# Squaring the MLP's features twice on ScalarE, and scaling the second pair of each group on VectorE, in a one-step hybrid diffusion layer

## The chip, the cores and the metric

The kernel runs on one core of a Trainium2 chip. The metric is the device time of one execution in microseconds (us); lower is better. Times from several runs are given as a median.

## What is computed

One transformer-like layer is run for two groups of tokens that share the weights: 512 latent tokens and 128 context tokens, 640 in all, each of width 1024. The layer has a modulated norm, a combined projection, two parallel head groups (mLSTM and latent attention), an output projection, and an MLP. The change lies in the MLP alone:

```python
h2 = _rmsnorm(x, norm2_g) * (1 + sc2) + sh2
x = x + g2 * (jnp.square(jax.nn.relu(h2 @ w_mlp_up)) @ w_mlp_down)   # 1024 -> 4096 -> 1024
```

## The kernel before

Tokens lie along the free dimension and features along the 128 partitions, so a block of 128 features of all tokens is a tile of 128x640, worked on in two halves of 320 tokens. All data are float32. A matmul operand is written as a high part (rounded to `fp32r`) and a low part (what the rounding left), and a product is three matmul passes: high by high, high by low, low by high.

The MLP goes through 4096 hidden features in 8 groups (`g`) of two pairs (`p = 2g` and `2g + 1`); a pair is two blocks of 128 features. For each pair `up_pair` forms the up product by a seven-product scheme (M1 to M7, each 12 matmuls of 128x322 in `product`, line 1232). Each product lands in one of four small PSUM buffers, and VectorE adds it into the pair's tiles `r1`, `r2`, `u` (line 1248; M1 is copied by ScalarE, line 1253). A PSUM buffer is free for a later product only when VectorE has read it.

`up_out` (lines 1265 to 1277) then makes the pair's features, half block by half block, four of them in a pair. The token's norm factor is multiplied in on GpSimd (line 1270), ScalarE adds the bias and applies relu (line 1274, one or two instructions, since the two token groups have different biases), ScalarE squares into the high part `fh` (line 1275), VectorE squares the same tile in place at full precision (line 1276), and VectorE subtracts the high part from that to get the low part `fl` (line 1277).

When both pairs of a group are there, eight down tiles `dn` of 24 matmuls each follow (line 634, called from the loop at the end), and VectorE adds them into the residual (`gated`, lines 1115 to 1117). The first of the eight takes all terms with `fh` first and those with `fl` last (`low_last`). The first products of the next group's pair are placed in between.

Weights come by DMA on SyncE's queue; each is split into its high part on ScalarE (line 109) and its low part on VectorE (line 110). GpSimd also forms the sums `S` of weight quarters that the seven-product scheme wants (line 219). So VectorE, ScalarE and GpSimd each have one queue, in order, in which feature work, weight work and PSUM reading share the places.

The order in each queue isn't the order of the code: the tile framework schedules the whole program at build time by a timeline of its own, and it may also alternate the matmuls of two products that are open at the same time. A change of engine therefore moves neighbours too.

Of the kernel before, what the change touches and what calls it, by code (L numbers as in the profile page):

```python
# [13 lines left out]
AF = mybir.ActivationFunctionType  # L14
ALU = mybir.AluOpType
# [39 lines left out]
def hybrid_layer(ctx: ExitStack, tc: tile.TileContext, d, o):  # L55
    nc = tc.nc
    V, S, G, PE = nc.vector, nc.scalar, nc.gpsimd, nc.tensor
# [17 lines left out]
    def U(name, dt=F32):  # L75
        return upool.tile([P, UNIT], dt, tag="u", name=name)
# [12 lines left out]
    def Tt(name, dt=F32, n=T):  # L89
        t = tp.tile([P, 646], dt, tag="t", name=name)  # L90
        return t[:, :n]
# [13 lines left out]
    def f(ap):  # L105
        return ap.bitcast(F32)
# [238 lines left out]
    for what in ORD:  # L345
        if what == "x":
            i = state["x"]
            nc.sync.dma_start(out=x3[i // 2][:, 2 * (i % 2):2 * (i % 2) + 2], in_=d["x"][:, 2 * i:2 * i + 2])
            state["x"] += 1
        elif what == "a":  # L350
            t = view(U(f"ad{len(adu)}"), 0, 4, 512)
# [111 lines left out]
    for g in range(4):  # L463
        if g:
            ada_first(g)
        if g == 1:
            rbs = Tt("rb1")
# [57 lines left out]
    for i in range(NT):  # L525
# [7 lines left out]
                      in_=st[:, KL + ROPE:KL + ROPE + 8].rearrange("p (a b) -> p a b", a=2))  # L533
        V.tensor_copy(out=gf[:, i, :].rearrange("p (a b) -> p a b", a=2)[:, :, 0:4],
                      in_=st[:, KL + ROPE + 8:KL + ROPE + 16].rearrange("p (a b) -> p a b", a=2))
# [48 lines left out]
    for ci, row in enumerate((r_a, r_e, r_w)):  # L584
        nt = NT if ci < 2 else 4
        pc = psS(f"pcol{ci}")
        for i in range(nt):
            PE.transpose(out=pc[:, i * 64:(i + 1) * 64], in_=row[:, i * P:(i + 1) * P], identity=ident[0:64, 0:64])
        V.tensor_copy(out=cols[:, ci, 0:nt].rearrange("p t d h -> p (t d) h"),
                      in_=pc[:, 0:nt * 64].rearrange("p (t b) -> p t b", b=32)[:, :, 0:4])  # L590
# [8 lines left out]
    for w in range(2):  # L599
# [4 lines left out]
                        in1=gs.unsqueeze(1).broadcast_to([P, NT, 2, 16]), op=ALU.mult)  # L604
# [195 lines left out]
    for k in range(2):  # L800
        pt = psD(f"ckt{k}")
        for i in range(NT):
# [17 lines left out]
                    in0=krn[:, 0:4].rearrange("p t (a b) -> p t a b", a=2)[:, :, ::-1, :],  # L820
                    in1=sg_[:, 1, 0:4].rearrange("p t (a b) -> p t a b", a=2), op=ALU.mult)
# [9 lines left out]
    for hf in range(2):  # L831
# [7 lines left out]
        for i in range(6):  # L839
            ps = psD(f"kvu{hf}{i}")[:, 0:512]  # L840
            for k in range(2):
                c = slice(k * 512, (k + 1) * 512)
# [13 lines left out]
        for i in range(6):  # L856
            G.tensor_tensor(out=kn[:, i, :, 0:NOPE], in0=kn[:, i, :, 0:NOPE], in1=rsk[:, i, :].unsqueeze(2).broadcast_to([P, 4, NOPE]), op=ALU.mult)
            G.tensor_tensor(out=kn[:, i, :, NOPE:QK], in0=krr[:, i:i + 1, :].broadcast_to([P, 4, ROPE]),
                            in1=rsk[:, i, :].unsqueeze(2).broadcast_to([P, 4, ROPE]), op=ALU.mult)
# [12 lines left out]
    for hf in range(2):  # L872
# [4 lines left out]
        for i in range(NT):  # L877
            ps = (psS if i % 2 else psD)(f"qu{hf}{i}")
            for k in range(3):
                hi, lo = w0 if k < 2 else w1  # L880
                c = slice((k % 2) * QL, (k % 2) * QL + QL)
# [7 lines left out]
            if i < 4:  # L889
                rt = view(Pp(f"rt{hf}{i}"), 0, 4, ROPE)  # L890
                V.tensor_tensor(out=rt.rearrange("p h (a b) -> p h a b", a=2),
                                in0=p4[:, :, NOPE:QK].rearrange("p h (a b) -> p h a b", a=2)[:, :, ::-1, :],
                                in1=sg_[:, 0, i:i + 1, :].rearrange("p t (a b) -> p t a b", a=2).broadcast_to([P, 4, 2, 16]), op=ALU.mult)
# [260 lines left out]
    for m in OUT_ORDER:  # L1154
# [19 lines left out]
        if m < 4:  # L1174
            osplit("B11", m, z1)
            t = Pp(f"t1{m}", n=SW)
            G.tensor_tensor(out=t, in0=z2, in1=z1, op=ALU.subtract)
            osplit("T1", m, t)
        else:
            k = m - 4  # L1180
            E = V if k == 3 else G
            t = Tt(f"t32{m}", n=2 * SW)
            t3, t2 = t[:, 0:SW], t[:, SW:2 * SW]
            c = TL - HT
# [52 lines left out]
    held = {}  # L1237
# [24 lines left out]
            if p == 0 and name == "M7":  # L1262
                add("M5", m5)

    def up_out(r, rbs, FH, FL):

        for n, hf in ((0, 0), (1, 1), (1, 0), (0, 1)):
            c = slice(hf * HT, (hf + 1) * HT)
            t = r[n][:, 2 + hf * HT:2 + (hf + 1) * HT]
            G.tensor_tensor(out=t, in0=t, in1=rbs[:, c], op=ALU.mult)  # L1270
            for w, (c0, c1) in enumerate(((0, TL), (TL, T))):
                c0, c1 = max(c0 - hf * HT, 0), min(c1 - hf * HT, HT)
                if c1 > c0:
                    S.activation(out=t[:, c0:c1], in_=t[:, c0:c1], func=AF.Relu, bias=r[n][:, w:w + 1])  # L1274
            S.activation(out=FH[n][:, c], in_=t, func=AF.Square)  # L1275
            V.tensor_tensor(out=t, in0=t, in1=t, op=ALU.mult)  # L1276
            V.tensor_tensor(out=FL[n][:, c], in0=t, in1=f(FH[n][:, c]), op=ALU.subtract)  # L1277

    feats = {}
    for g in range(NG):  # L1280
        if g < NG - 1:
            feats[g] = kview([U(f"fh{g}", F32R)] * 2)[:4], kview([U(f"fl{g}", F32R)] * 2)[:4]
        else:
            feats[g] = [], []
        FH, FL = feats[g]
        for i in range(2):
            p = 2 * g + i
            up_pair(p, LATER if i == 0 and g else ORDER0 if p == 0 else ORDER[AHEAD:] if p == 1 else ORDER)
            if p == 0:
                up_pair(1, ORDER[:AHEAD])  # L1290
                rbs = norm2(sums2())
            if g == NG - 1:
                u = U("f0", F32R) if i == 0 else U2(php, "f1", F32R)
                for k in range(2):
                    FH.append(view(u, k * T, T))
                    FL.append(view(u, (2 + k) * T, T))
            up_out(held.pop(p)[:2], rbs, FH[2 * i:2 * i + 2], FL[2 * i:2 * i + 2])
        if g < NG - 1:
            up_pair(2 * g + 2, ORDER[:PRE])
        for h, m2 in downs(g):  # L1300
            w = wnext(("down", h, m2))
            for m in (2 * m2, 2 * m2 + 1):
                ps = psD(f"dn{h}{m}")
                c = (m % 2) * 512
                w_ = [t[:, c:c + 512] for t in w]
                if (h, m) == (NG - 1, KT - 1):

                    for hf in range(2):
                        mmT(ps, w_, *feats[h], 4, hfs=(hf,))
                else:  # L1310
                    mmT(ps, w_, *feats[h], 4, low_last=(h, m) == (g, 0))
                gated(ps, m, 40)
                if h == NG - 1:
                    cuts = (0, HT, T) if m == KT - 1 else (0, T)
                    for c0, c1 in zip(cuts, cuts[1:]):
                        (S if c0 == 0 else nc.sync).dma_start(out=o["y"][m][:, c0:c1], in_=xr[m][:, c0:c1])
# [95 lines left out]
```

## Time and profile before

| what | us |
|---|---|
| median of 3 runs (894.12 to 899.8) | 894.95 |
| the profiled execution, its own time | 894.66 |
| span of the profile (first to last instruction) | 892.8 |
| PE busy in the span | 852.2 |
| DVE busy in the span | 633.5 |
| ACT busy in the span | 414.6 |
| POOL busy in the span | 340.4 |

In the rows PE is TensorE's matmul, DVE is VectorE, ACT is ScalarE and POOL is GpSimd. A number at the head of a row is its start in us from the start of the span. A duration reaches from an instruction's start to its last write, and instructions that follow each other on one engine overlap by some tens of ns, so what one costs its queue is the distance between starts. "x12" is twelve instructions of one kind in a row. Idle time before an instruction, and what ended it, stand in square brackets. A matmul's duration contains its way through the array: 310 ns for one, while the next starts after about 147 ns, so idle time under 150 ns does not show as idle.

### The profile page before, as it was taken

The page shows a single profiled execution, that of the slowest core. Times are in us where ns is not written, and L with a number is a line of the kernel's source. Part 1 is how long each engine was busy: PE and PEld are TensorE (multiplying, and loading weights), DVE is VectorE, ACT ScalarE, POOL GpSimd, SP SyncE. Part 2 cuts the span into 40 slices and gives each one's busy share as a digit, 9 for nine tenths or more (in the row PEclk, how much of TensorE's full clock was granted, in tenths as well). Part 3 has the DMA queues.
Part 4 walks back from the last instruction along what each step waited for, and adds up shares of the span by engine and source line. Part 5 has one row for each costly group of instructions (what it writes and reads, how often), then busy time and mean ns, then how long its engine had stood idle before and what let it go on. Part 6 is the DMA issues. An engine that isn't in the chain of part 4 may idle for free.

```text
span 892.8 us, 15207 instructions
## 1 busy us (share of the span) xinstructions
PE 852.2 (95%) x5775; PEld 794.2 (89%) x5775; DVE 633.5 (71%) x1260; ACT 414.6 (46%) x895; POOL 340.4 (38%) x343
## 2 busy tenths in 40 slices
PE   3999999999889999999989999999999999999998
PEld 2688889999778677889989999999999999999998
DVE  3654634546787789968899587694976949678673
ACT  3424426436864688946556143341534415243430
POOL 3100113313334567734654354352624427254320
PEclk9999999999999999999999999999999999999999
DMA  9742742231226100322131312222132221412122
GB/s 357 315 130 76 288 157 90 64 97 51 95 77 239 73 1 1 119 71 84 48 130 38 104 48 95 71 71 96 48 103 86 72 72 51 137 50 71 49 98 91
DMA packets 22329, 89.64 MB, mean 100 GB/s; under 512 B 3144, under 2 KB 3944, under 8 KB 18928
## 3 DMA queue, kind: packets, MB, share of 16 engines
q1 hardware_dynamic: 19440, 81.95, 26.4%
q0 software_dynamic: 1664, 4.26, 1.6%
q10 hardware_dynamic: 1152, 2.46, 0.7%
q8 instruction: 46, 0.75, 0.3%
q14 instruction: 27, 0.22, 0.1%
HBM read 85.33 MB, written 3.32 MB: 99 GB/s over the span
## 4 chain that ended last, share of the span: by engine, by line
PE 67%; DVE 17%; DMA 6%; issue 5%; ACT 3%; POOL 1%; SPq 1%; DVEq 0%; POOLq 0%; ACTq 0%
PE dn L634 23%; PE qk L634 6%; PE wo L634 5%; DVE wu L110 3%; DMA st<-in_w_ada 3%; DVE r L1276 3%; PE mo L634 2%; PE pv L1010 2%; DMA ad<-in_w_ada 2%; DVE r L1248 2%; DVE fl L1277 2%; PE ada L389 2%; PE n L699 1%; PE up8M L1232 1%; PE up14M L1232 1%
## 5 line engine op out<-in xcount | busy, mean ns | idle before, releaser
L1270 POOL TENSOR_TENSOR r<-r,rbs 128x320 f32<-128x320 f32 x64 | 76.9, 1215 | 120.1 <-DVE r L1248 120.1
L109 ACT CAST wh<-st 128x1024 fp32r<-128x1024 f32 (+4 forms) x69 | 69.4, 1009 | 106.1 <-PE dn L634 40.4
L1115 DVE SCALAR_TENSOR_TENSOR xr<-dn,modT,xr 128x320 f32<-128x320 f32 x64 | 35.2, 550 | 106.8 <-PE dn L634 106.8
L634 PE MATMUL dn<-fl,wh 128*128 128x320 f32 x448 | 100.4, 311 | 4.0 <-DVE fl L1277 4.0
L634 PE MATMUL dn<-fh,wh 128*128 128x320 f32 x448 | 103.4, 310 | 0.0
L634 PE MATMUL dn<-fh,wl 128*128 128x320 f32 x448 | 102.0, 309 | 0.0
L110 DVE TENSOR_TENSOR wl<-st,wh 128x1024 fp32r<-128x1024 f32 (+4 forms) x67 | 82.2, 1229 | 24.5 <-ACT wh L109 23.5
L109 ACT CAST wu<-S 128x512 fp32r<-128x512 f32 x64 | 37.6, 617 | 108.0 <-issue 46.7
L634 PEld LDWEIGHTS dn<-fl,wh 128*128 128x128 f32 x448 | 74.1, 188 | 5.8 <-DVE fl L1277 5.8
L634 PEld LDWEIGHTS dn<-fh,wh 128*128 128x128 f32 x448 | 75.5, 188 | 0.5 <-PE dn L634 0.2
L634 PEld LDWEIGHTS dn<-fh,wl 128*128 128x128 f32 x448 | 74.9, 188 | 0.0
L1274 ACT ACTIVATE r<-r 128x192 f32<-128x192 f32 (+2 forms) x96 | 40.9, 464 | 40.4 <-DVE r L1248 27.9
L110 DVE TENSOR_TENSOR wu<-S,wu 128x512 fp32r<-128x512 f32 x64 | 54.5, 860 | 1.1 <-ACT wu L109 0.9
L1276 DVE TENSOR_TENSOR r<-r 128x320 f32<-128x320 f32 x64 | 45.7, 731 | 0.6 <-ACT fh L1275 0.6
L726 POOL TENSOR_TENSOR W<-ngb,mask 128x128 f32<-128x128 f32 x40 | 19.3, 496 | 69.1 <-DVE p L736 30.9
L1001 POOL TENSOR_TENSOR tot<-tot,p 128x512 f32<-128x512 f32 x24 | 37.2, 1548 | 5.9 <-ACT p L983 3.9
L219 POOL TENSOR_TENSOR S<-st,st 128x512 f32<-128x512 f32 x8 | 13.5, 1683 | 60.5 <-DVE wu L110 60.5
L110 DVE TENSOR_TENSOR pu<-p,pu 128x512 fp32r<-128x512 f32 x32 | 33.1, 1049 | 2.5 <-ACT pu L109 2.5
L109 ACT CAST wu<-pair 128x512 fp32r<-128x512 f32 x24 | 14.1, 615 | 43.6 <-PE dn L634 41.4
L1277 DVE TENSOR_TENSOR fl<-r,fh 128x320 fp32r<-128x320 f32 x56 | 33.3, 613 | 0.2
L1010 PE MATMUL pv<-pu,v 128*128 128x512 f32 x80 | 29.1, 427 | 2.3 <-DVE pu L110 2.0
L219 POOL TENSOR_TENSOR S<-pair 128x512 f32<-128x512 f32 x16 | 26.6, 1659 | 12.0 <-DVE wu L110 8.2
(485 smaller groups left out, 2416.6 us busy)
## 6 DMA issues: line engine op xcount, KB each, us to landing
st<-in_w_ada SPq DMA_DIRECT2D x16, 1024.0 KB, 5.6
st<-in_w_down SPq DMA_DIRECT2D x32, 512.0 KB, 3.3
ad<-in_w_ada SPq DMA_DIRECT2D x8, 1024.0 KB, 16.6
st<-in_w_up SPq DMA_DIRECT2D x16, 512.0 KB, 3.7
pair<-in_w_up SPq DMA_DIRECT2D x16, 512.0 KB, 4.8
st<-in_w_qko SPq DMA_DIRECT2D x12, 512.0 KB, 3.5
st<-in_w_out SPq DMA_DIRECT2D x8, 512.0 KB, 3.6
x<-in_x SPq DMA_DIRECT2D x4, 640.0 KB, 6.9
```

The costliest lines, as they stand in the source:

```text
L109: S.copy(hi, src)
L110: return eng.tensor_tensor(out=lo, in0=src, in1=f(hi), op=ALU.subtract)
L219: G.tensor_tensor(out=t, in0=a, in1=b, op=op)
L634: PE.matmul(out[:, hf * 512:hf * 512 + HT], lhsT=wt[:, c], rhs=xt[k][:, hf * HT:(hf + 1) * HT], start=k0 == 0 and n == 0, stop=k1 == nk an ...
L726: G.tensor_tensor(out=W[:, dg:dg + P], in0=nb_[dr][:, j * P:(j + 1) * P], in1=mask[:, dr, :], op=ALU.add)
L1001: G.tensor_tensor(out=tot[h], in0=first, in1=pj, op=ALU.add)
L1010: PE.matmul(pacc[h], lhsT=v_u[hf][:, j, hh_, :], rhs=w, start=j == 0 and k == 0, stop=j == 4 and k == 1)
L1115: V.scalar_tensor_tensor(out=xr[m][:, 0:HT], in0=ps[:, 0:HT], scalar=modT[:, gi_ + m, 0:1], in1=xr[m][:, 0:HT], op0=ALU.mult, op1=ALU.add)
L1270: G.tensor_tensor(out=t, in0=t, in1=rbs[:, c], op=ALU.mult)
L1274: S.activation(out=t[:, c0:c1], in_=t[:, c0:c1], func=AF.Relu, bias=r[n][:, w:w + 1])
L1276: V.tensor_tensor(out=t, in0=t, in1=t, op=ALU.mult)
L1277: V.tensor_tensor(out=FL[n][:, c], in0=t, in1=f(FH[n][:, c]), op=ALU.subtract)
```

## The change

The full-precision square moves from VectorE to ScalarE, in all 16 pairs. The multiplication by the token factor stays on GpSimd for the first pair of each group and moves to VectorE for the second.

```diff
-    def up_out(r, rbs, FH, FL):
+    def up_out(r, rbs, FH, FL, E):
...
-            G.tensor_tensor(out=t, in0=t, in1=rbs[:, c], op=ALU.mult)
+            E.tensor_tensor(out=t, in0=t, in1=rbs[:, c], op=ALU.mult)
...
             S.activation(out=FH[n][:, c], in_=t, func=AF.Square)
-            V.tensor_tensor(out=t, in0=t, in1=t, op=ALU.mult)
+            S.activation(out=t, in_=t, func=AF.Square)
             V.tensor_tensor(out=FL[n][:, c], in0=t, in1=f(FH[n][:, c]), op=ALU.subtract)
...
-            up_out(held.pop(p)[:2], rbs, FH[2 * i:2 * i + 2], FL[2 * i:2 * i + 2])
+            up_out(held.pop(p)[:2], rbs, FH[2 * i:2 * i + 2], FL[2 * i:2 * i + 2], V if i else G)
```

The build-time schedule is the same up to the first features and differs from there. Three places of the third group (`g = 2`, pairs 4 and 5) follow; the other groups but the first read alike.

VectorE's queue where the second pair's features are finished, before: `r15` and `r25` are the second pair's tiles, `up5M3` is its last product, `wl` are weight low parts, `r16`, `r26`, `u6` belong to the next pair.

```order
L1248 TENSOR_TENSOR r15_6245<-r15_6245,up5M3_6363 128x322
L110 TENSOR_TENSOR wl114_6404<-st114_6271,wh114_6403 128x1024
L1276 TENSOR_TENSOR r25_6246<-r25_6246 128x320
L1276 TENSOR_TENSOR r15_6245<-r15_6245 128x320
L1276 TENSOR_TENSOR r25_6246<-r25_6246 128x320
L1277 TENSOR_TENSOR fl2_6162<-r25_6246,fh2_6161 128x320
L1277 TENSOR_TENSOR fl2_6162<-r15_6245,fh2_6161 128x320
L1277 TENSOR_TENSOR fl2_6162<-r25_6246,fh2_6161 128x320
L1248 TENSOR_TENSOR u6_6401<-r16_6399,up6M6_6422 128x322
L110 TENSOR_TENSOR wl115_6438<-st115_6273,wh115_6437 128x1024
L1276 TENSOR_TENSOR r15_6245<-r15_6245 128x320
```

The same place in VectorE's queue after the change:

```order
L1270 TENSOR_TENSOR r15_6245<-r15_6245,rbs_5137 128x320
L1270 TENSOR_TENSOR r25_6246<-r25_6246,rbs_5137 128x320
L1248 TENSOR_TENSOR r15_6245<-r15_6245,up5M3_6363 128x322
L110 TENSOR_TENSOR wl114_6404<-st114_6271,wh114_6403 128x1024
L1270 TENSOR_TENSOR r15_6245<-r15_6245,rbs_5137 128x320
L1277 TENSOR_TENSOR fl2_6162<-r25_6246,fh2_6161 128x320
L1248 TENSOR_TENSOR u6_6401<-r16_6399,up6M6_6422 128x322
L110 TENSOR_TENSOR wl115_6438<-st115_6273,wh115_6437 128x1024
L1277 TENSOR_TENSOR fl2_6162<-r15_6245,fh2_6161 128x320
L1277 TENSOR_TENSOR fl2_6162<-r25_6246,fh2_6161 128x320
```

The squares are gone from the queue and the factor products stand in it, three of the pair's four ahead of the weight split `wl114` and one right behind it.

ScalarE's queue at the end of the same pair, after the change: `wh` are weight high parts, line 1274 is relu, line 1275 the square into `fh`, line 1276 the new square, line 1253 the next pair's M1 copy.

```order
L1275 ACTIVATE fh2_6161<-r25_6246 128x320
L1276 ACTIVATE r25_6246<-r25_6246 128x320
L1253 COPY r16_6399<-up6M1_6402 128x322
L109 CAST wh115_6437<-st115_6273 128x1024
L1276 ACTIVATE r15_6245<-r15_6245 128x320
L1274 ACTIVATE r15_6245<-r15_6245 128x192
L1276 ACTIVATE r25_6246<-r25_6246 128x320
L1274 ACTIVATE r15_6245<-r15_6245 128x128
L109 CAST wh116_6471<-st116_6407 128x1024
L1275 ACTIVATE fh2_6161<-r15_6245 128x320
L1276 ACTIVATE r15_6245<-r15_6245 128x320
```

Three of the new squares and a weight cast (`wh116`) now stand ahead of the group's last `fh` (next to last row); before, no square and no `wh116` did.

TensorE's queue where the last low part is first read (`dn20`, `fl2`, x3), before; 16 matmuls of `dn20` with `fh2` stand ahead of these rows.

```order
L634 MATMUL dn20_6475<-fl2_6162,wh114_6403 128x320 x5
L634 MATMUL dn21_6503<-fh2_6161,wh114_6403 128x320
L634 MATMUL dn20_6475<-fl2_6162,wh114_6403 128x320 x3
L634 MATMUL dn21_6503<-fh2_6161,wh114_6403 128x320
L634 MATMUL dn21_6503<-fl2_6162,wh114_6403 128x320 x2
```

The same after the change; 19 matmuls of the group (9 of `dn20`, then 10 of `dn21` on the first pair's features) stand ahead of these rows.

```order
L634 MATMUL dn20_6475<-fh2_6161,wh114_6403 128x320
L634 MATMUL dn20_6475<-fh2_6161,wl114_6404 128x320 x2
L634 MATMUL dn20_6475<-fh2_6161,wh114_6403 128x320 x2
L634 MATMUL dn20_6475<-fh2_6161,wl114_6404 128x320 x2
L634 MATMUL dn20_6475<-fl2_6162,wh114_6403 128x320 x5
L634 MATMUL dn21_6503<-fh2_6161,wl114_6404 128x320 x2
L634 MATMUL dn21_6503<-fh2_6161,wh114_6403 128x320 x2
L634 MATMUL dn21_6503<-fl2_6162,wh114_6403 128x320
L634 MATMUL dn20_6475<-fl2_6162,wh114_6403 128x320 x3
L634 MATMUL dn21_6503<-fl2_6162,wh114_6403 128x320
```

The first reading of the group's last `fl` moves from behind 22 matmuls of the group's down tiles to behind 36; that of the last `fh` (the first row of this piece) from behind 9 to behind 19.

## Rows read from the trace of the kernel before

**Rows 1.** The page, busy time of the engines over the span.
```profile
PE 852.2 (95%) x5775; PEld 794.2 (89%) x5775; DVE 633.5 (71%) x1260; ACT 414.6 (46%) x895; POOL 340.4 (38%) x343
```

**Rows 2.** Chain that ended last, from 440 us: start, us, what.
```profile
517.48 0.55 DVE xr L1115
...
789.76 0.55 DVE xr L1115
...
841.15 12.47 PE up15M L1232 x84
853.62 35.21 PE dn L634 x240
```

**Rows 3.** Timeline of PE, third group, 586 to 600 us: start, us.
```profile
586.48 1.94 PE L1232 MATMUL up5M<-B,wu 128*128 128x322 f32 x12
588.57 2.01 PE L1232 MATMUL up6M<-B,wu 128*128 128x322 f32 x12 [0.16 <-DVE r L1248]
590.54 5.59 PE L1232 MATMUL up6M<-T,wu 128*128 128x322 f32 x36
595.97 0.45 PE L634 MATMUL dn<-fh,wh 128*128 128x320 f32 x2
...
599.12 0.31 PE L634 MATMUL dn<-fh,wh 128*128 128x320 f32 x1
599.86 0.71 PE L634 MATMUL dn<-fl,wh 128*128 128x320 f32 x3 [0.43 <-DVE fl L1277]
```

**Rows 4.** Timeline of PE, first group, at its last low part.
```profile
491.09 0.31 PE L634 MATMUL dn<-fl,wh 128*128 128x320 f32 x1
492.75 0.86 PE L634 MATMUL dn<-fl,wh 128*128 128x320 f32 x4 [1.34 <-DVE fl L1277]
```

**Rows 5.** Waits of PE from 463 us on: us in total, times, longest.
```profile
PE dn L634 <- DVE fl L1277: 4.0, 7, 1.3
```

**Rows 6.** Windows: busy us of each engine (instructions), clock, DMA share, GB/s.
```profile
571.97:602.41 30.44, 29.85 (x198) 29.09 (x197) 30.40 (x48) 16.88 (x35) 17.53 (x13) 1.00 0.21 69
602.41:626.41 24.00, 24.00 (x166) 24.00 (x165) 10.72 (x25) 3.59 (x6) 4.72 (x3) 1.00 0.27 89
```

**Rows 7.** Groups by line, 440 to 893 us: busy us, mean ns | idle before.
```profile
L1270 POOL TENSOR_TENSOR r<-r,rbs 128x320 f32<-128x320 f32 x64 | 76.9, 1215 | 120.1 <-DVE r L1248 120.1
...
L1276 DVE TENSOR_TENSOR r<-r 128x320 f32<-128x320 f32 x64 | 45.7, 731 | 0.6 <-ACT fh L1275 0.6
...
L109 ACT CAST wh<-st 128x1024 fp32r<-128x1024 f32 x32 | 33.7, 1053 | 50.6 <-PE dn L634 40.4 <-DMA st<-in_w_down 5.2 <-PE up15M L1232 0.6
```

**Rows 8.** Line 1276, 517 to 790 us: shortest/median/longest ns.
```profile
L1276 DVE TENSOR_TENSOR r<-r x40: 476/481/1584, 524.7 to 761.9; 128x320 f32<-128x320 f32 x40
```

**Rows 9.** Timeline of DVE, third group.
```profile
573.02 0.68 DVE L110 TENSOR_TENSOR wu<-S,wu 128x512 fp32r<-128x512 f32 x1
573.62 0.48 DVE L1248 TENSOR_TENSOR r<-r,up4M 128x322 f32<-128x322 f32 x1
...
576.19 1.38 DVE L110 TENSOR_TENSOR wu<-st,wu 128x512 fp32r<-128x512 f32 x1
577.50 0.47 DVE L1248 TENSOR_TENSOR r<-r,up4M 128x322 f32<-128x322 f32 x1
...
591.61 0.88 DVE L1248 TENSOR_TENSOR r<-r,up5M 128x322 f32<-128x322 f32 x2
...
599.33 0.47 DVE L1277 TENSOR_TENSOR fl<-r,fh 128x320 fp32r<-128x320 f32 x1
```

**Rows 10.** Timeline of POOL, third group.
```profile
575.28 1.74 POOL L219 TENSOR_TENSOR S<-st,S 128x512 f32<-128x512 f32 x1
```

**Rows 11.** Timeline of ACT, third group.
```profile
592.18 1.21 ACT L1274 ACTIVATE r<-r 128x192 f32<-128x192 f32 x3 [4.46 <-DVE r L1248]
...
594.11 0.82 ACT L1275 ACTIVATE fh<-r 128x320 fp32r<-128x320 f32 x2
...
596.73 0.47 ACT L1275 ACTIVATE fh<-r 128x320 fp32r<-128x320 f32 x1
```

## The prediction

> **What bounds the kernel now.** First the page's busy times: TensorE works 852.2 of 892.8 us [rows 1]. That already says that no change on another engine can bring much; only TensorE's holes can be closed. Then the chain that ended last, to see how large the holes are. The residual additions at 517.48 and 789.76 us close the same step of five groups that read alike, so a group takes (789.76 - 517.48) / 5 = 54.46 us. It holds 14 up products of 12 matmuls (168) and 8 down tiles of 24 (192). Where nothing holds TensorE up, 84 up matmuls take 12.47 us and 240 down matmuls 35.21 us [rows 2], which is 148.5 and 146.7 ns each. So a group's matmuls alone are 168 x 0.1485 + 192 x 0.1467 = 53.11 us, and 1.35 us of a group is waiting.
>
> Where they sit is in TensorE's timeline [rows 3]. Read the distances between starts, since much of it is too short to show as idle. From 586.48 to 588.57 twelve up matmuls take 2.09 us in place of 1.78: 0.31 lost, and the row names VectorE's reading of PSUM. The next twelve take 1.97 (0.19 lost), the 36 behind them 5.43 in place of 5.35 (0.08). The 21 down matmuls from 595.97 take 3.15 in place of 3.08 (0.07). One matmul at 599.12 holds its place for 0.74 (0.59 lost): the row behind it waits for VectorE's last low part. That is 1.24 us of the 1.35. In the list of waits the low part has 4.0 us in seven waits [rows 5]: 1.34 in the first group [rows 4] and some 0.44 in each of six more. The first group's down matmul at 491.09 is followed at 492.75, so 1.51 us are lost there. The eighth group runs its 240 without a hole [rows 2].
>
> The cause is one queue. From 571.97 to 602.41 VectorE is busy 30.40 of 30.44 us, while ScalarE has 16.88 and GpSimd 17.53 [rows 6]. Behind that block both the PSUM reads and the last features come late; in the other 24.00 us VectorE has 10.72 of work.
>
> **The change part by part.** *The square leaves VectorE.* It was 45.7 us for 64, 0.71 each, eight in a group: 5.7 us off the block [rows 7]. Its bare cost is nearer to its median of 481 ns, some 0.40 between starts; the longest took 1584 [rows 8], so the relief is between 3.2 and 5.7 us. I take 5.7, since those long ones did stand in the queue.
>
> *The factor product comes onto VectorE*, four in a group. No row shows it there. Its nearest row is the square itself, with the same 128x320 in and out: at least 0.40 us from start to start, at most 1.58. I take 0.48, the median [rows 8], because GpSimd loses exactly those four products, of 1.2 us each [rows 7], that ran beside that part of the queue: 1.9 us, with ends of 1.6 and 6.3. That GpSimd matters for VectorE is in the rows: a 128x512 subtraction costs 0.60 us from start to start at 573.02 and 1.31 at 576.19 [rows 9], where GpSimd was in the middle of a sum that ended at 575.28 + 1.74 = 577.02 [rows 10]; VectorE went on 0.48 us behind that end.
>
> The Trainium skill (State Buffer, Who interferes with whom) calls this an exclusive lock: a VectorE instruction with two SBUF inputs and a GpSimd one that reads SBUF exclude each other for a whole instruction. The trace agrees, with those 0.48 us behind the end at 577.02. By it a moved product could be held for one sum, 1.74 us [rows 10]; once in a group, that would leave 2.1 of the 3.8 us that the next sentence finds.
>
> So VectorE's block loses 5.7 - 1.9 = 3.8 us of its 30.4, and 1.35 us of TensorE's waiting hang on it; by the ends it loses 5.7 - 1.6 = 4.1 or gains 6.3 - 3.2 = 3.1. What would be late next?
>
> *ScalarE gets the eight squares.* The square into the high part is the same function on the same shape: two take 0.82 us [rows 11], so one costs at most 0.41. That is 3.3 us on 16.88 of 30.44. The four of the first pair lie in front of a hole of 4.46 us, which ends at 592.18 with the second pair's relu [rows 11], so they cost nothing. Of the second pair's, three come ahead of the group's last high part, 1.2 us, and with them one weight cast more, 1.05 us [rows 7]. But the chain in front starts earlier: before, VectorE read the last product of the pair at about 592.0 [rows 9] though TensorE had finished it by 588.57 [rows 3], and GpSimd needed 1.2 us more for its factor. With the block shorter by 3.8 us VectorE reads it at 588.6 to 589, and the factor takes 0.5. That is 3 to 4 us earlier, against 2.3 us more on ScalarE.
>
> *TensorE's order moves too.* The group's last low part, ready at 599.33 + 0.47 = 599.80 before [rows 9], is first read behind 36 matmuls of the down tiles in place of 22. With the up stalls (0.31 + 0.19 + 0.08) closed the first of these starts at 595.97 - 0.58 = 595.4, so it is wanted at 595.4 + 36 x 0.147 = 600.7: even a low part that came no earlier than now would be in time by 0.9 us. The last high part, ready at 596.73 + 0.47 = 597.20 [rows 11], is wanted behind 19, at 598.2. Both have slack before anything gets faster. GpSimd and the DMAs only lose work or keep theirs.
>
> *The sum.* Six groups (second to seventh) lose 1.35 each, of which I leave 0.15 as small hand-overs between ScalarE, PSUM and TensorE (bounds 0 and 0.5): 6 x 1.20 = 7.2 us. The first group loses its 1.51, with bounds 0 and 1.7: 1.5 us. The rest is the same to the instruction. Profiled execution: 894.66 - 8.7 = 885.96; it stood 0.29 us under the median, so the forecast is 886.3 us.
>
> **The rivals.**
> *The moved product buys nothing.* A factor product on VectorE would cost what it cost GpSimd, 1.2 us, four times 4.8, and the relief is 5.7 - 4.8 = 0.9 us. For it speaks the 1.31 in place of 0.60 [rows 9]; against it, that GpSimd no longer does the very work that collides. Of each group's 1.35 some 0.45 stays, 0.30 more than in the forecast, and of the first group's 1.5 some 0.6: 886.3 + 6 x 0.30 + 0.6 = 888.7 us. The Trainium skill (Perfetto Trace Analysis, Optimizing Scalar/DVE Operations) warns of this: work moved between GpSimd and VectorE may not help, as they share an SBUF read port; this trace agrees as to the sharing, and that rule alone would give this case.
>
> *TensorE's holes are not VectorE's.* The releasers are inferred, and the high parts or the weight casts may be what ended the waits. Then 1 us or so goes: 894. Against it: VectorE's 30.40 of 30.44.
>
> *ScalarE becomes the late one (slower).* The place is the group's last high part. If all eight squares and the cast end up ahead of it on the path, 8 x 0.41 + 1.05 = 4.3 us, it comes at 601.5 where 598.2 is wanted: a stall of 3.3 us in place of 1.35, in seven groups 14 us: about 909. It begins to lose where the high part is 1.0 + 1.35 = 2.35 us later than now. Against it stand the 4.46 us hole and the earlier start. The far end of the factor product's price (a block longer by 3.1 us) would end on the same side.
>
> **How the numbers follow.** Forecast 0.66 (its own range 884.5 to 888.0), the moved product that buys nothing 0.18, holes that are not VectorE's 0.11, ScalarE late 0.05. The floor is all holes closed, 894.95 - 6 x 1.35 - 1.7 = 885.2, and 0.7 for the spread of a measurement: 884.5. The range goes up through the second case and to the edge of the third, 892.5. Below 1% of a difference, 8.95 us, a measurement of this kernel tells little, and the bound is 886.0: the forecast lies right above it. About half of its 0.66 falls under it, so faster 0.33, within 1% 0.62, slower 0.05. The direction is far surer than the 1%.
>
> **What would show it.** Right: groups of 53.2 to 53.4 us between the residual additions; VectorE's block ending some 3 us earlier or showing idle time; no wait of the down tiles for low parts in the steady groups, and the twelve matmuls ahead of the second pair's end at 1.8 us. The factor product on VectorE with a median near 0.48 us. Wrong: groups near 54.4; or TensorE waiting for ScalarE's high part; or the factor product near 1.2 us.

## The result and the profile after

The changed kernel takes 889.79 us (median of 9 runs, 885.95 to 892.8) against 895.2 us for the kernel before (9 runs, 893.61 to 899.8) on the same chip: a ratio of 0.9929 with a 95% interval of 0.9911 to 0.9946 (worked out from all the runs; the two medians alone give 0.994). It is faster by 0.7%, which is within the 1% that the prediction set as its bound. Run again beside the experiments, it gave 888.13 us (6 runs, 887.41 to 889.06), ratio 0.9909 [0.9888, 0.9931]. The profiled execution took 886.72 us, where the prediction's sum for it was 885.96. The 3 us between it and the median lie within the spread of the runs, over 6 us in either kernel, which goes in part with the clock that TensorE was granted (last section).

The page, busy time of the engines:

```profile
PE 850.2 (96%) x5775; PEld 795.8 (90%) x5775; DVE 617.5 (70%) x1228; ACT 436.9 (49%) x959; POOL 300.8 (34%) x311
```

Against [rows 1], ScalarE has 64 instructions more, VectorE and GpSimd 32 fewer each: 64 squares and 32 products moved, as the diff says. TensorE has the same 5775 matmuls.

The chain that ended last, after the change (start, us, what):

```profile
458.13 2.04 PE up1M L1232 x12
...
572.69 12.47 PE up5M L1232 x84
585.16 7.12 PE up6M L1232 x48
592.28 17.84 PE dn L634 x120
...
626.02 12.47 PE up7M L1232 x84
...
749.68 4.19 DMA st<-in_w_down
...
753.95 1.05 ACT wh L109
...
833.22 12.47 PE up15M L1232 x84
```

Where [rows 2] left TensorE for VectorE once in every group, the chain now stays on TensorE: 84 up matmuls, 48 more, 120 down matmuls, with nothing between them. A group takes 626.02 - 572.69 = 53.33 us, where it took 54.46. `up15M` starts at 833.22, 7.93 us earlier than in [rows 2]; 0.51 of that lie ahead of the MLP's first feature, since the `up1M` row stood at 458.64 before (row in the last section). One group is 0.6 longer (53.96): its weight cast `wh` at 753.95 waited for the DMA that landed at 749.68 + 4.19 = 753.87, and the group's last `fh` stood behind the cast.

TensorE's timeline in the third group (start, us, in brackets the idle time and what ended it):

```profile
583.21 1.95 PE L1232 MATMUL up5M<-B,wu 128*128 128x322 f32 x12
585.00 1.93 PE L1232 MATMUL up6M<-B,wu 128*128 128x322 f32 x12
586.76 5.51 PE L1232 MATMUL up6M<-T,wu 128*128 128x322 f32 x36
592.12 0.45 PE L634 MATMUL dn<-fh,wh 128*128 128x320 f32 x2
...
597.26 0.90 PE L634 MATMUL dn<-fl,wh 128*128 128x320 f32 x5
...
598.87 0.45 PE L634 MATMUL dn<-fh,wl 128*128 128x320 f32 x2
599.33 0.53 PE L634 MATMUL dn<-fh,wh 128*128 128x320 f32 x2
599.70 0.46 PE L634 MATMUL dn<-fl,wh 128*128 128x320 f32 x2
```

The places that lost time in [rows 3] are at their bare price: twelve up matmuls take 585.00 - 583.21 = 1.79 us, then 1.76, and 36 take 5.36. The last low parts are read in the row at 597.26 without a wait. What is left stands around 599.33: the two matmuls at 598.87 hold their place for 0.46 us and the next two for 0.37 instead of 0.29 each, 0.25 us in all. The row at 599.33 begins with the first matmul of the third down tile, and VectorE has just emptied the first tile's PSUM buffer (its last read of it ends at 599.18).

TensorE's list of waits from 463 us on, where [rows 5] had 4.0 us for the low part alone:

```profile
PE dn L634 <- ACT fh L1275: 0.3, 1, 0.3
```

Now the engine that was to be relieved. The window of one steady group, before and after (us of the window, then busy us of PE, PEld, DVE, ACT and POOL with their instructions, clock, DMA share, GB/s):

```profile
571.97:626.43 54.46, 53.87 (x362) 53.10 (x361) 41.14 (x73) 20.49 (x41) 22.25 (x16) 1.00 0.24 78
```

```profile
568.70:622.04 53.34, 53.34 (x362) 53.11 (x361) 39.77 (x69) 23.35 (x49) 17.12 (x12) 1.00 0.24 80
```

VectorE lost eight squares and gained four products, for which the prediction took 3.8 us off. It fell by 41.14 - 39.77 = 1.37 us only (1.46 on average over four groups). The groups of VectorE's instructions over four groups of the MLP say where the rest is (busy us, mean ns of one | idle before). Before, 517.48 to 735.31 us:

```profile
L110 DVE TENSOR_TENSOR wu<-S,wu 128x512 fp32r<-128x512 f32 x32 | 26.5, 839 | 0.0
L1276 DVE TENSOR_TENSOR r<-r 128x320 f32<-128x320 f32 x32 | 23.6, 757 | 0.0
...
L1277 DVE TENSOR_TENSOR fl<-r,fh 128x320 fp32r<-128x320 f32 x32 | 18.8, 605 | 0.1
...
L110 DVE TENSOR_TENSOR wu<-pair,wu 128x512 fp32r<-128x512 f32 x12 | 10.6, 914 | 0.0
```

After, 515.30 to 728.70 us:

```profile
L110 DVE TENSOR_TENSOR wu<-S,wu 128x512 fp32r<-128x512 f32 x32 | 29.7, 937 | 0.0
L1277 DVE TENSOR_TENSOR fl<-r,fh 128x320 fp32r<-128x320 f32 x32 | 22.1, 711 | 1.7 <-ACT r L1276 1.7
...
L110 DVE TENSOR_TENSOR wu<-pair,wu 128x512 fp32r<-128x512 f32 x12 | 12.8, 1092 | 0.0
...
L1270 DVE TENSOR_TENSOR r<-r,rbs 128x320 f32<-128x320 f32 x16 | 7.4, 481 | 0.0
```

The squares' 23.6 us are gone and the products cost 7.4, at 481 ns each. But three neighbours of the same size and number as before grew: the splits by 3.2 and 2.2 us and the low parts by 3.3, 8.7 us in four groups or 2.2 in one. (Per group that leaves (23.6 - 7.4 - 8.7) / 4 = 1.9 us of durations; the busy time falls by less, since durations overlap by some 0.08 us from one instruction to the next and there are four instructions fewer.)

In the same traces one can lay VectorE's instructions beside GpSimd's. Before, 12 of the 32 squares ran beside a GpSimd instruction and took 1220 ns on average; the other 20 took 480, none more than 483. Of the 32 low parts 12 ran beside one, at 816 ns before and 1089 after the change, and the others took 479 and 484. In the steady groups of every run of this document, squares, factor products, low parts and weight splits with no GpSimd instruction beside them keep one duration for their shape to within 11 ns. So what these lines cost above that is waiting for GpSimd. It is 7.1 us in a group before and 7.0 after the change: the squares that waited are gone, and the waiting is not.

The features came hardly earlier. VectorE's timeline after the change:

```profile
585.28 1.60 DVE L110 TENSOR_TENSOR wu<-S,wu 128x512 fp32r<-128x512 f32 x1
...
587.21 0.88 DVE L1270 TENSOR_TENSOR r<-r,rbs 128x320 f32<-128x320 f32 x2
588.02 0.48 DVE L1248 TENSOR_TENSOR r<-r,up5M 128x322 f32<-128x322 f32 x1
...
596.00 1.04 DVE L1277 TENSOR_TENSOR fl<-r,fh 128x320 fp32r<-128x320 f32 x1
```

And ScalarE's last `fh` of the same pair:

```profile
594.08 0.47 ACT L1275 ACTIVATE fh<-r 128x320 fp32r<-128x320 f32 x1
```

VectorE reads the pair's last product at 588.02, 3.02 us after TensorE went on to the next one (585.00); before, it was 592.01 against 588.57, 3.44 us. The last `fh` is ready at 594.08 + 0.47 = 594.55, 2.43 us after the first down matmul (592.12); before it was 597.20 against 595.97, 1.23 us. The last `fl` is ready at 596.00 + 1.04 = 597.04, 4.92 us after it; before 599.80, 3.83 us. Measured from where TensorE begins the down tiles, both features are later than before by more than a microsecond, and yet TensorE doesn't wait. Why is what the experiments are about.

### The profile page after: what moved, and what is told of

Read it like the earlier page. It is cut to its first block, busy times and chain, and to the rows that moved or that the text cites. A ratio compares the mean times of both kernels' runs of the same rounds, so it can differ in the third digit from the quotient of the medians.

```text
span 884.9 us, 15161 instructions
## 1 busy us (share of the span) xinstructions
PE 850.2 (96%) x5775; PEld 795.8 (90%) x5775; DVE 617.5 (70%) x1228; ACT 436.9 (49%) x959; POOL 300.8 (34%) x311
## 4 chain that ended last, share of the span: by engine, by line
PE 82%; DVE 8%; DMA 4%; ACT 3%; issue 2%; POOL 0%; SPq 0%; DVEq 0%; POOLq 0%; ACTq 0%
PE dn L634 25%; PE qk L634 6%; PE wo L634 5%; PE mo L634 2%; PE ada L389 2%; PE pv L1010 2%; PE n L699 1%; PE up4M L1232 1%; PE up8M L1232 1%; PE up9M L1232 1%; PE up13M L1232 1%; PE up15M L1232 1%; PE up14M L1232 1%; PE up7M L1232 1%; PE up5M L1232 1%
## 5 line engine op out<-in xcount | busy, mean ns | idle before, releaser
L1270 POOL TENSOR_TENSOR r<-r,rbs 128x320 f32<-128x320 f32 x32 | 38.8, 1224 | 106.6 <-DVE r L1248 106.6
L110 DVE TENSOR_TENSOR wu<-S,wu 128x512 fp32r<-128x512 f32 x64 | 58.6, 925 | 1.1 <-ACT wu L109 0.9
L1277 DVE TENSOR_TENSOR fl<-r,fh 128x320 fp32r<-128x320 f32 x56 | 38.2, 700 | 3.0 <-ACT r L1276 3.0
L634 PE MATMUL wo<-mh,wh 128*128 128x320 f32 x128 | 29.6, 311 | 0.7 <-DVE xr L1117 0.7
L634 PE MATMUL qk<-hh,wh 128*128 128x320 f32 x128 | 30.0, 314 | 0.0
```

The costliest lines, as they stand in the source:

```text
L110: return eng.tensor_tensor(out=lo, in0=src, in1=f(hi), op=ALU.subtract)
L634: PE.matmul(out[:, hf * 512:hf * 512 + HT], lhsT=wt[:, c], rhs=xt[k][:, hf * HT:(hf + 1) * HT], start=k0 == 0 and n == 0, stop=k1 == nk an ...
L1270: E.tensor_tensor(out=t, in0=t, in1=rbs[:, c], op=ALU.mult)
```

## The experiments

The first theory is the prediction's: TensorE's 1.35 us of waiting per group hang on VectorE's full queue, and its relief closes them. The rivals: only one of the two moves counts; or the relief is worth little and what closes the holes is TensorE's own order, in which the build-time schedule now lets the second down tile's matmuls run ahead of the last features. The kernels change engines and the order of matmuls only. "Group" is the distance between the first up matmuls of pairs 3, 5, 7, 9 and 11, the same place four times; the granted clock is 1.00 over all of these groups.

**The changed kernel again.** No edit; it stands beside the next three.

> The changed kernel as it is, on the same chip as its parts. Theory (one queue: TensorE's 1.35 us of waiting per group hung on VectorE's backlog, and the change closed all but 0.24): ratio to the kernel before 0.990 to 0.994, groups of 53.3 us between residual additions. Rival (the time of the changed kernel is set by TensorE's granted clock, which was below full for 3.4 us just ahead of the first up products of its profile while that of before was full throughout): its runs scatter between 886 and 893 with their granted clock, and so do those of the kernel before; then the best runs of both differ by 7 to 8 us and the medians by less.

888.13 us, ratio 0.9909 [0.9888, 0.9931]; groups of 53.37 and 53.33 us in turn, the later one with the late weight cast 54.03. So the trace above repeats.

**The square alone.** The factor product stays on GpSimd for both pairs:

```diff
-up_out(..., V if i else G)
+up_out(..., G)
```

> Only the square moves to ScalarE; all factor products stay on GpSimd. Theory (one queue, and any relief above 1.35 us a group is as good as more): 5.7 us a group leave VectorE, none come; the waits of the down tiles for low parts go, ratio 0.990 to 0.995, like the whole change. Rival (the two parts add up, each in proportion to what it takes off VectorE or the chain): a part of the gain, and the second pair's factor products still late on GpSimd, ratio 0.995 to 0.998 with a wait for low parts of 0.2 us or more left in each group.

891.65 us (12 runs), ratio 0.9957 [0.9938, 0.9976]; groups of 53.98 to 54.05. The ratio lies in the rival's range; the theory that any relief above 1.35 us is as good as more has failed. The window of a group and, over four groups (519.32 to 735.36), VectorE's line of low parts:

```profile
573.38:627.36 53.98, 53.64 (x362) 53.09 (x362) 39.45 (x64) 23.13 (x49) 21.61 (x16) 1.00 0.24 79
```

```profile
L1277 DVE TENSOR_TENSOR fl<-r,fh 128x320 fp32r<-128x320 f32 x32 | 24.7, 781 | 3.5 <-ACT r L1276 3.5
```

This is the cleanest look at the first wrong term. Eight squares, 23.6 / 4 = 5.9 us of a group, leave VectorE, nothing comes in, and VectorE falls by 41.14 - 39.45 = 1.69 us. The low parts went from 605 to 781 ns on average: 20 of the 32 now run beside a GpSimd instruction, where 12 did. The weight splits grew too. The long squares had been waiting behind GpSimd; without them the next instructions in the queue meet GpSimd's and wait in their place, 8.3 us in a group where it was 7.1. About half of the change's gain is here, and TensorE still waits six times for a low part (2.0 us in all, at most 0.3).

**The factor product alone.** The square goes back to VectorE, the second pair's factor product stays there:

```diff
-S.activation(out=t, in_=t, func=AF.Square)
+V.tensor_tensor(out=t, in0=t, in1=t, op=ALU.mult)
```

> Only the second pair's factor products move to VectorE; the squares stay there. VectorE gets 1.9 us a group more of bare work and loses the collisions with four GpSimd products. Theory (one queue, collisions with GpSimd counted in it): the collisions weigh about as much as the added work, VectorE's block is about as long as before, and the chain is shorter by some 0.7 us per product; ratio 0.994 to 1.000. Rival (a moved product buys nothing, VectorE's queue is simply longer): block longer by 1.9 us, waits of over 1.35 us a group, ratio 1.002 to 1.015.

894.22 us (12 runs), ratio 0.9979 [0.9959, 0.9998]; groups of 53.82 to 53.87, one of 54.60.

```profile
629.26:683.12 53.86, 53.70 (x362) 53.15 (x362) 41.14 (x76) 20.58 (x40) 16.67 (x12) 1.00 0.24 79
```

The mirror image: four products come onto VectorE, 4 x 0.48 = 1.9 us, and in this window it is as busy as before, 41.14 us (41.53 in the group ahead of it). GpSimd lost 5.6 us of work, and the waits of VectorE's instructions behind it fell from 7.1 to 5.6 us in a group, about what VectorE took over. The low part is no longer waited for, but TensorE waits for VectorE's PSUM reads, once for 0.9 us. Its gain of 0.21% and the square's 0.43% stand against 0.91% for the whole, timed beside them.

**All factor products on VectorE.**

```diff
-up_out(..., V if i else G)
+up_out(..., V)
```

> The square on ScalarE and the factor products of both pairs on VectorE. Theory (one queue with slack left after the change): VectorE has 2 to 3 us of slack in a group, so four more products of 0.40 us cost nothing and the first pair's collisions go too: ratio within 0.002 of the changed kernel's. Rival (the split by pairs is at an optimum, VectorE is again the late one when it gets all): waits for low parts return, 0.3 us or more a group, ratio 0.002 to 0.005 above the changed kernel's.

886.98 us (6 runs), ratio 0.9899 [0.9875, 0.9923]; groups of 53.33 to 53.36, the one behind the late cast included, and no wait on TensorE's list.

```profile
572.46:625.79 53.33, 53.33 (x362) 53.10 (x362) 39.02 (x72) 23.09 (x49) 11.64 (x8) 1.00 0.24 80
```

Four more products on VectorE, and it is less busy by 0.75 us than in the changed kernel: the waits behind GpSimd fell to 4.8 us in a group. Its interval overlaps the changed kernel's: as good, perhaps a little better.

**The change with the down tiles in turn.** All engines as in the changed kernel, but the second down tile's matmuls may stand in TensorE's queue only behind the first tile's last, as they did before but for one matmul in each group. The last `fh` is read behind 9 matmuls again and the last `fl` behind 21:

```diff
+elif (h, m) == (g, 1):
+    with tc.issue_after(dn0.ins):
+        mmT(ps, w_, *feats[h], 4)
...
-mmT(ps, w_, *feats[h], 4, low_last=(h, m) == (g, 0))
+dn0 = mmT(ps, w_, *feats[h], 4, low_last=(h, m) == (g, 0))
```

> The changed kernel with TensorE's order of before: the second down tile of a group is issued behind the last matmul of the first, so the last low part is read behind 22 matmuls again. VectorE's queue is the same to the row. In the changed kernel's trace the last low part is there 4.9 us after the first down matmul (597.04 against 592.12); in the trace of before it was 3.8 us (599.80 against 595.97). Theory (the shorter queue closed the up stalls, but the new order of TensorE hides the low part): TensorE reaches it 3.2 us after the start and waits some 1.4 to 1.7 us in each group and 0.1 to 0.3 for the last high part, while the up stalls stay closed: a group of 54.5 to 55.0 us and a ratio of 0.998 to 1.004. Rival (the shorter queue alone pays): ratio 0.990 to 0.994 as in the changed kernel.

899.67 us (9 runs) against 894.79: ratio 1.0056 [1.0035, 1.0076], slower than the kernel before. Groups take 55.08 to 55.12 us, slightly more than the theory's 55.0. The longest entry of TensorE's list of waits in it (line numbers are one higher here; us in total, times, longest):

```profile
PE dn L634 <- ACT fh L1276: 6.9, 6, 1.9
```

Its timeline in the fourth group:

```profile
645.81 1.95 PE L1233 MATMUL up7M<-B,wu 128*128 128x322 f32 x12
647.61 1.93 PE L1233 MATMUL up8M<-B,wu 128*128 128x322 f32 x12
...
654.72 0.46 PE L634 MATMUL dn<-fh,wh 128*128 128x320 f32 x2
...
655.90 0.31 PE L634 MATMUL dn<-fh,wh 128*128 128x320 f32 x1
657.01 0.41 PE L634 MATMUL dn<-fh,wh 128*128 128x320 f32 x1 [0.80 <-ACT fh L1276]
...
658.14 0.90 PE L634 MATMUL dn<-fl,wh 128*128 128x320 f32 x5
659.68 0.71 PE L634 MATMUL dn<-fl,wh 128*128 128x320 f32 x3 [0.65 <-DVE fl L1278]
```

And when those features were made, on ScalarE and VectorE:

```profile
656.49 0.47 ACT L1276 ACTIVATE fh<-r 128x320 fp32r<-128x320 f32 x1
...
658.59 1.04 DVE L1278 TENSOR_TENSOR fl<-r,fh 128x320 fp32r<-128x320 f32 x1
```

The last `fh` is ready 656.49 + 0.47 - 654.72 = 2.24 us after the first down matmul and the last `fl` 4.91 us: the features come where they came in the changed kernel (2.43 and 4.92). The up matmuls don't wait (647.61 - 645.81 = 1.80 us for twelve). Only the reading moved, and TensorE loses 0.96 us at 655.90 (1.11 in place of 0.15) and 0.81 at 658.14 (1.54 in place of 5 x 0.147), and 0.1 more behind each. That is nearly all of the 1.99 us that this group has above the 53.11 of its matmuls alone; the changed kernel has 0.23, at the third down tile, where this one doesn't wait. So the moved work by itself makes the features late, and what keeps the changed kernel from paying is the order of TensorE's queue.

**The kernel before with the changed kernel's order.** Engines as before; the matmuls of the first two down tiles are written out in the order in which the changed kernel's queue has them:

```diff
+for m, n in ((0, 9), (1, 10), (0, 12), (1, 5), (0, 3), (1, 9)):
+    part = (d0, d1)[m][at[m]:at[m] + n]
...
+        with tc.issue_after(last.ins):
+            last = emit()
```

> The kernel of before, squares on VectorE and all factor products on GpSimd, with the changed kernel's order of the first two down tiles written out. Theory (the order hides the low part, the queue sets the up stalls): the wait for low parts, 0.6 to 0.7 us a group, goes; the stalls of the up products (0.58) stay and 0.2 come for the PSUM buffer of the third tile: a group of 53.9 to 54.1 us, ratio 0.995 to 0.997. Rival (the shorter queue alone pays): ratio 0.999 to 1.002.

892.94 us (12 runs), ratio 0.9979 [0.9961, 0.9996]; groups of 53.90 to 53.95. Its timeline:

```profile
640.91 1.95 PE L1232 MATMUL up7M<-B,wu 128*128 128x322 f32 x12
643.00 2.00 PE L1232 MATMUL up8M<-B,wu 128*128 128x322 f32 x12
...
657.15 0.46 PE L1293 MATMUL dn<-fh,wl 128*128 128x320 f32 x2
657.61 0.54 PE L634 MATMUL dn<-fh,wh 128*128 128x320 f32 x2
```

The 0.59 us for the low part are gone, the up matmuls lose what they lost before (twelve take 2.09 in place of 1.78), and the third tile's short wait at 657.15 is there. The groups are the theory's, the ratio falls short of its 0.995 to 0.997; the first group still waits 1.4 us for its low part. With this and the run before, a steady group stands at

| us per group | TensorE's order before | order of the changed kernel |
|---|---|---|
| engines before | 54.46 | 53.92 |
| engines of the change | 55.10 | 53.34 |

In these groups the two kernels of a row have the same instructions in the same order on VectorE, ScalarE and GpSimd, and the two of a column have TensorE's matmuls in the same order but for the one named above. Neither part does it. The order alone saves 0.54 us, the moved work alone costs 0.64, and both save 1.12. The moved work frees the PSUM reads (the 0.58 us of up stalls) but makes the last features later than the old order could bear.

**A weave that leaves the third tile no wait.** All factor products on VectorE and an order in which the first down tile ends earlier, its last low part read behind 32 matmuls instead of 36 (the edit is against the order of the last experiment):

```diff
-((0, 9), (1, 10), (0, 12), (1, 5), (0, 3), (1, 9))
+((0, 9), (1, 10), (0, 12), (1, 1), (0, 3), (1, 13))
```

> Square on ScalarE, factor products of both pairs on VectorE, and the first down tile finished four matmuls earlier than in the changed kernel (its last low part read behind 32). Theory (the 0.24 us left in each group is TensorE waiting at the third down tile until VectorE has emptied the first one's PSUM buffer, because the two woven tiles end close together): the two long steps there, 0.31 and 0.22 us, fall to 0.15, a group takes 53.1 us in place of 53.33, and the ratio is 0.987 to 0.990. Rival (those steps are something else, such as the weights of the third tile): they stay and the ratio is that of the kernel with all factor products on VectorE, 0.990.

885.77 us (6 runs), ratio 0.9902 [0.9877, 0.9928]; groups of 53.12 and 53.09 us, which is the 53.11 of the matmuls alone. The ratio is the one that the rival named too; the groups and the steps at the third tile decide for the theory:

```profile
651.62 0.46 PE L1293 MATMUL dn<-fh,wl 128*128 128x320 f32 x2
651.92 0.46 PE L634 MATMUL dn<-fh,wh 128*128 128x320 f32 x2
```

The third tile's first matmul (651.92) follows after 0.30 us, two matmuls at their bare price: 13 matmuls of the second tile now stand behind the end of the first, in which VectorE empties its buffer. The version above with the same engines had groups of 53.33 to 53.36, so this wait was what is left in it, and in the changed kernel.

**The same weave with the changed kernel's engines, and the version above again.**

> The changed kernel's engines (factor products of the second pair alone on VectorE) with the first down tile finished four matmuls earlier, as in the woven kernel before it. Theory (the 0.24 us a group is the wait for the first tile's PSUM buffer, and the last low part of the changed kernel comes 4.9 us behind the first down matmul, just when it is read behind 32): the two long steps at the third tile go, and 0 to 0.3 us of waiting for the last low part come in their place: a group of 53.1 to 53.4 us, ratio 0.989 to 0.993. Rival (reading it earlier brings back a stall as long as with the tiles in turn): a group of 53.8 us or more, ratio 0.994 or more.

> The woven kernel with all factor products on VectorE once more, beside the kernel above on one chip. Theory (it leaves TensorE nothing to wait for in the steady groups): groups of 53.1 us and the best time of all kernels here, ratio 0.987 to 0.991. Rival (nothing is gained against the changed kernel's own order): ratio 0.991 or more.

Timed together, beside the kernel before at 897.92 us (11 runs): the changed kernel's engines with this weave take 889.04 us (6 runs), ratio 0.991 [0.9883, 0.9937], groups of 53.47 to 53.50; with all factor products on VectorE 884.78 us (5 runs), ratio 0.9876 [0.9849, 0.9902], groups of 53.09 and 53.12. In the first of the two, TensorE's timeline has

```profile
652.44 0.31 PE L1293 MATMUL dn<-fh,wl 128*128 128x320 f32 x1
652.86 0.71 PE L1293 MATMUL dn<-fl,wh 128*128 128x320 f32 x3
```

One matmul holds its place for 0.42 us in place of 0.15, and the next row loses 0.1 more: reading the low part 4 matmuls earlier brought its wait back, larger than the 0.25 us that it saved, and the groups are above the 53.4 expected. The order has to fit when the features come. With all factor products on VectorE it fits, and that version has the shortest groups here; its time is below the kernel before by 1.0% and 1.2% on two occasions. It was not timed side by side with the changed kernel, and the times don't set it apart from the kernel with all factor products on VectorE in the scheduler's own order (0.9899).

## Why the prediction was right, and which steps failed

*The time.* The median of 889.79 us lies inside the stated range (884.5 to 892.5), but 3.5 us above the forecast of 886.3 and above the 888.0 at which the forecast's own range ends; the second timing, 888.13, lies just above that end. By time alone the rival in which the moved product buys nothing (888.7) would be nearer. The groups decide against it: it left 0.3 us more in each.

*What bounds the kernel, and the size of the gain.* Right. The groups were to be 53.2 to 53.4 us and are 53.34: 1.12 us saved, where 1.20 was taken. The first group was to lose 1.5 us of waiting; the next pair's weight loads stand 2.1 us earlier, 0.51 of which lie ahead of the first group, which leaves 1.6. (Those are the weight loads of `up3M` for the operand `T`, from 522.9 to 520.8 us. Those of `up13M`, five groups on, went from 795.2 to 788.1.) The five groups between give 7.1 - 2.1 = 5.0 us: five times 1.12 less 0.6 for the late weight cast. The rest of the way to `up15M` gives 0.8. So the profiled execution fell by 894.66 - 886.72 = 7.94 us, where the sum had 8.7: 0.6 less for the late cast, 0.4 less in the five groups at 1.12 instead of 1.20, 0.4 less in the last stretch, 0.1 more in the first group, and the 0.5 ahead of it, which the sum did not have.

*The 0.15 us left per group for small hand-overs, bounds 0 and 0.5.* It is 53.34 - 53.11 = 0.23, and it is one hand-over, the PSUM buffer of the third down tile.

*The factor product at 0.48 us.* Right: median 481 ns, shortest 478, longest 488 over 20 of them.

*VectorE's block loses 3.8 us.* This term failed. It was the squares' 5.7 us, priced by their mean, less 1.9. Measured: 1.37 us. The mean of 0.71 contained the waits behind GpSimd, and the prediction took them as going away with the squares, "since those long ones did stand in the queue". They were handed on: the neighbours grew by 2.2 us a group. Priced bare, at the 0.40 us between starts that the prediction kept as the other end, the sum is 3.2 - 1.6 = 1.6 us, near to what was measured. That it comes so near is a balance of two shifts that the bare price leaves out: the square alone takes off 1.69 where it would be 3.2, for the most part because VectorE's waits behind GpSimd grew by 1.2 us, and the factor products alone add 0 to 0.4 where they would add 1.6, because these waits fell by 1.5. The Trainium skill (SBUF — State Buffer, Who interferes with whom) says that a VectorE instruction with two SBUF inputs and a GpSimd one that reads SBUF shut each other out for a whole instruction; the traces agree, in that VectorE's instructions of this kind are long only beside a GpSimd one (low parts with none beside them took 484 ns, the others 1089, in the changed kernel), and the square alone (605 to 781 ns for an unchanged low part) adds that the price belongs to the meeting and not to the instruction that happens to be there. It isn't a constant either: with the same VectorE queue the four groups have 39.05 to 40.14 us of VectorE in the changed kernel and 39.00 to 39.02 with the tiles in turn, where only TensorE's order differs.

*"That is 3 to 4 us earlier, against 2.3 us more on ScalarE."* This step failed with it. VectorE reads the last product 0.4 us earlier against TensorE (3.02 us behind it, from 3.44), not 3 to 4: ahead of that read stand a split that takes 1.60 us and two of the moved products. ScalarE's squares and the extra weight cast came in full: ScalarE works with hardly a pause from the second pair's first relu at 587.32 to 595.05, and so the last `fh` is 1.2 us later and the last `fl` 1.1 us later than before, counted from the first down matmul. Of the signs that the prediction named, idle time in VectorE's block did come (0.42 us ahead of 590.46, 0.37 ahead of 591.72); an end 3 us earlier did not.

*TensorE's order.* This step carried the result. It said that the last features would be wanted behind 19 and 36 matmuls instead of 9 and 22, and gave the slack for a low part that came no earlier. By the measured times the last `fh` is wanted at 592.12 + 19 x 0.147 = 594.91 and ready at 594.55, the last `fl` is wanted at 597.41 and ready at 597.04: 0.36 and 0.37 us to spare. The prediction listed it as a safety; with the tiles in turn it proves to be the whole difference between 0.7% faster and 0.6% slower. So the forecast of the groups came out with two of its steps wrong, and that is in part luck: the prediction had reckoned this slack for features no later than before, they came more than 1 us later, and it just sufficed. What did come from VectorE's relief is the up stalls.

*The rivals.* "The moved product buys nothing" had the wrong price for the product (1.2 us against 0.48), but was near to VectorE's total relief (0.9 forecast, 1.4 measured); TensorE's holes closed all the same. The Trainium skill (Perfetto Trace Analysis, Optimizing Scalar/DVE Operations) cautions that moving work between these two engines might not help, since they share an SBUF read port. The factor product alone agrees with it as to the sharing (VectorE's time stayed about as it was, and GpSimd's fell by 5.6 us), and the kernel became 0.2% faster all the same, by an interval that just excludes no change. "TensorE's holes are not VectorE's" falls for the up stalls, which stayed when only the order changed or only the products moved, and went when the squares left; the low part's wait went by the order alone. "ScalarE becomes the late one" had the right place, the group's last high part, and the right engine, with 6.9 us of waits when the tiles are in turn; its 14 us were too many even there (5 us by the medians), and the order hid it.

*What remains open.* The single moves add up to 0.64% of the whole's 0.91%; the intervals reach some 0.2% to either side, so the times don't say whether the rest is an interaction of the two. The groups show it better, but each of these kernels also has an order of its own for TensorE, which was not held fixed.

## What to carry to other kernels

Price work that leaves a shared resource by its bare (median) duration at most, not by its mean: the waits in the mean belong to whoever meets the other engine, and the next instruction inherits them. In this kernel these waits grew when VectorE alone was relieved, and shrank when work left GpSimd, the engine that it met. When a producer in a tight pipeline gets more to do, count how many of the consumer's instructions stand ahead of its first use of the result; ten to fourteen matmuls of another open accumulation put in between decided here whether 1.4 us taken off the queue that looked full gained 0.7% or lost 0.6%. And test a move with the order held fixed, since a scheduler that reorders neighbours can be where the gain, or the loss, comes from.

## What was not expected of the hardware

The granted clock differs from run to run, and a good part of the spread in time goes with it. Of the runs of the kernel before that were timed beside the first experiments, four with a mean clock of 0.993 took 897.75 to 899.77 us, and two with 1.0 took 893.87 and 894.52; of the changed kernel's first nine, two with 0.993 took 892.13 and 892.8, one with 1.0 took 885.95. So at a like clock the change is worth 5 to 9 us. The clock doesn't account for everything: the profiled execution and another with the same 0.998 took 886.72 and 890.19 us. In the profiled execution of the changed kernel such a piece can be seen, just where the MLP begins (window, then TensorE's row in it):

```profile
453.70:457.50 3.80, 3.77 (x15) 3.75 (x15) 3.80 (x7) 1.68 (x4) 1.98 (x2) 0.55 0.05 20
```

```profile
453.74 2.91 PE L1232 MATMUL up0M<-B,wu 128*128 128x322 f32 x10 [1.89 <-ACT r L1253]
```

The granted clock is 0.55 over these 3.8 us, so most of them were at 1.2 GHz, and ten matmuls take 2.91 us. TensorE had been idle for 1.89 us. In the kernel before the same ten follow on the same idle time:

```profile
454.25 1.74 PE L1232 MATMUL up0M<-B,wu 128*128 128x322 f32 x10 [1.86 <-ACT r L1253]
...
458.64 1.75 PE L1232 MATMUL up1M<-B,wu 128*128 128x322 f32 x10 [0.70 <-DVE wu L110]
```

They take 1.74 us at a granted clock of 1.00. Here the slower piece cost nothing in the end: both kernels wait for VectorE a little later, and `up1M` goes on at 458.13 and 458.64, as far apart as the two pieces began. The same pause in front of the same work was answered by a lower clock in one execution and not in the other; what decides it, these runs don't show.
